# Five small moves in a two-layer encoder trunk: a put-off GpSimd product, one more row transposition before a stage border, weight splits kept to odd steps for longer, and two changes of order

## The chip, the cores and the metric

The kernel runs on one core of a Trainium2 chip. The metric is the device time of one execution in microseconds (us). Shown are three runs of the kernel before (median 1502.16 us) and one profiled execution of it. The engines are named as in the profile: PE (matrix multiplications and transpositions), PEld (its weight loads), DVE (vector), ACT (scalar, activations), POOL (GpSimd) and SP (which here only starts transfers).

## The reference, cut to what matters

The trunk has two layers over 1024 tokens of width 1024, all in fp32. Layer 0 uses neighbourhood attention (mixer A), layer 1 grouped-query attention (mixer B); both have 16 query heads of width 64.

```python
# one layer
h    = rms_norm(x, g)
proj = h @ w_in                       # q, k, v and a gate of the branch's width
o    = mixer(q, k, v)                 # A: window of 8 x 16 keys plus a bias; B: 4 kv heads, rotary, all 1024 keys
x    = x + (o * silu(gate)) @ w_out
x    = x + sigmoid(rms_norm(x) @ w_gate) * (p[i] @ w_ple)
# after both layers
out  = rms_norm(x, g_final)
```

The product of `o` and the gate is where the first edit sits. The attention output is scaled by 1 / (row sums), and by the gate, and is then the left operand of the output projection.

## The kernel before, in words

**Products.** Each fp32 operand is split into a high half and a low half, and a product is three matmuls (high by high, high by low, low by high), recorded under line L322. A split takes an ACT copy (the high half) and a DVE subtraction (the low half). Weight blocks of 128 x 1024 are staged by SP into `wstage`, split by ACT at L231 and DVE at L236, and queued in an object `WQ`. Rows of activations are turned by four PE transpositions into one PSUM bank `t` (L504), which ACT copies to `HTh` (L505) and DVE subtracts to `HTl` (L506). `to_ht(pool, tile, rows, halves)` does this for one tile of 128 tokens, once per half of the row.

**Stages.** Mixer A runs from about 65 to 515 us, its dense stage (the output projection by seven half-size products after Strassen, then the gated embedding) to about 694, mixer B to about 1319 and the second dense stage to the end.

**Order of work.** The order on each engine is the order in which the program is written. Attention items are woven with projections ("dense" items). `post.add(n, f)` puts off `f` by `n` pulses, and one pulse passes per woven item; `post.tick()` counts. `later` does the same per attention step.

**The end of a head pair (edit 1).** `head_end` collects a pair of heads in `Y` (128 x 512), once for each half `hf` of the queries. Row sums are inverted, sent through memory and spread by SP (`rD`, `rb`). Then `fin` multiplies on GpSimd twice: `Y` by the gate `G` (L611) and `Y` by `rb` (L612). Eleven pulses later `split` makes the high half on ACT (L608) and the low half on DVE (L609), and two transfers store them; for `pair < 4` and `hf == 1`, `Y` is stored as it is after 13 pulses. In mixer A the same GpSimd queue holds, once per step of eight, L831 for `PTh` and for `PTl` (the products that mask the outer columns of the turned probabilities), for which PE's product `o<-PTh,V` and `o<-PTl,V` waits; also L773 (the bias of the next head) and the transfers of L680 that add weight blocks for the Strassen sums. For the last pair, `fin_last` does the products on DVE, and `hi` and `lo` write directly into `HTh` (L589) and `HTl` (L592); for `hf == 0` they are put off by 3 and 5 pulses (edit 2).

**Steps of mixer B (edit 3).** 128 steps `n`. A step does scores `s`, their minimum (DVE L1311), the exponential (ACT L1317), eight transpositions (L1329), whose banks ACT (L1331) and DVE (L1332) split; every even step does two steps' product with `V` (L322, `o<-PTh,V` and `o<-PTl,V`, eight matmuls each). `WQ.gate` is false in even steps up to step 111, so that no weight split is made there; from step 112 it is open. Late in mixer B, at L654, ACT evacuates the products `d` of the embedding projection.

**The dense stage (edit 4).** `strassen_out` holds a table `plan` that gives, for each tile product, the additions (`s12`, `s3`: two or four DVE instructions at L1487 to L1495), copies (`sh`, L1505; `sl`, L1509) and weight splits (`wh`, L1457; `wl`, L1461) made after it.

**The border to mixer B (edit 5).** The dense stage keeps a list `pend` of row halves still to be turned. What is left at its end is handed to mixer B, which turns one of them after every second of its first projection items, into its own pool `psT`. That pool takes over the PSUM banks of the dense stage's pool `ps_t`, so that its first transpositions wait for the DVE instruction that last read such a bank. The items there are `k` and `v` products of 24 matmuls each into `s` (L322), evacuated by ACT (L1249, L1255).

Of the kernel before, what the change touches and what calls it, by code (L numbers as in the profile page):

```python
# [16 lines left out]
ALU = mybir.AluOpType  # L17
# [31 lines left out]
QO = (4, 6)  # L49
AGE, LAG = 3, 3  # L50
YS = (11, 11)
YLOAD_A, YLOAD_B = 0, 118
OPEN3 = 5
ULOAD = 5
# [107 lines left out]
def trunk(ctx, tc, x, wts, rpb, gains, hgains, mask, sides, rope, gain0, out):  # L162
    nc = tc.nc
    sync, act, dve, pool, pe = nc.sync, nc.scalar, nc.vector, nc.gpsimd, nc.tensor
# [97 lines left out]
    WQ = Weights()  # L262
# [56 lines left out]
    post = Later()  # L319
# [195 lines left out]
    def head_end(sb, h, hf, rs, Ops, ylive, layer, gg, talloc):  # L515
        pair = h // 2
        b = (h % 2) * 64
        if h % 2 == 0:
            Y = sb.tile([128, 512], F32, name="Y", bufs=3 if layer == 0 else 2)
            rb = sb.tile([128, 512], F32, name="rb", bufs=2)  # L520
            r8 = sb.tile([128, 8], F32, name="r8", bufs=4)
            ylive[pair, hf] = (Y, rb, r8, {})
        Y, rb, r8, tail = ylive[pair, hf]
        yh = Y[b:b + 64]

        def join():
            dve.scalar_tensor_tensor(yh, Ops[0:64], 0.5, yh, op0=ALU.mult, op1=ALU.add)

        def rows():
            r8T = sb.tile([128, 32], F32, name="r8T", bufs=2)  # L530
            dve.transpose(r8T.rearrange("p (a c) -> p a c", a=4), r8[:, None].to_broadcast([128, 4, 8]))
            rD = dram.tile([8, 128], F32, name="rD", bufs=4)
            for b in range(4):
                post.add(DD[layer][1], lambda b=b: sync.dma_start(rD[:, 32 * b:32 * b + 32], r8T[32 * b:32 * b + 8]))
            for i in range(2):
                post.add(DD[layer][1], lambda i=i: sync.dma_start(
                    rb[64 * i:64 * i + 64], bass.AP(tensor=rD.tensor, offset=rD.offset + 512 * i, ap=[[0, 64], [1, 512]])))

        def spread():
            dve.tensor_copy(rb.rearrange("p (t j c) -> p t j c", t=4, j=2),  # L540
                            r8.rearrange("p (j t) -> p t j", j=2)[:, :, :, None].to_broadcast([128, 4, 2, 64]))

        def across():
            ps = talloc()
            for t in range(4):
                pe.transpose(ps[:, t], rb[:, t * 128:(t + 1) * 128], ident)
            ps = ps.rearrange("p t c -> p (t c)")
            if hf == 0:
                act.activation(rb, ps, AF.Copy)
            tail["rb"] = rb if hf == 0 else ps  # L550

        def norm():
            if "sums" in tail and h % 2:
                post.add(DT[hf], across)
                return
            dve.reciprocal(r8[:, 4 * (h % 2):4 * (h % 2) + 4], rs)
            if h % 2 == 0:
                return
            if pair < 7 or layer == 1 and hf == 0:
                post.add(DD[layer][0], rows)  # L560
                tail["rb"] = rb
            else:
                spread()
                post.add(DT[hf], across)

        def evac():
            act.activation(yh, Ops[64:128], AF.Copy, scale=0.5)
            post.add(DY, join)
            norm()
        if h == NH - 1 and hf == 1:  # L570
            evac()
        else:
            post.add(DO[layer], evac)
        if h % 2 == 0:
            return None
        G = gg.pop((pair, hf))
        del ylive[pair, hf]

        def fin_last():
            dve.tensor_tensor(Y, Y, G, ALU.mult)  # L580
            if "rb" not in tail:
                post.l = [e for e in post.l if e[1] is not across]
                across()
            dve.tensor_tensor(Y, Y, tail["rb"], ALU.mult)
            y3 = Y.rearrange("p (t c) -> p t c", t=4)
            ts = slice(4 * hf, 4 * hf + 4)

            def hi():
                act.activation(HTh[:, ts, 7, :], y3, AF.Copy)  # L589

            def lo():
                dve.tensor_tensor(HTl[:, ts, 7, :], y3, HTh[:, ts, 7, :], ALU.subtract)  # L592
            if hf == 0:
                post.add(3, hi)
                post.add(5, lo)
            else:
                hi()
                lo()

        def fin():  # L600
            yhi, ylo = rb.bitcast(F32R), Y.bitcast(F32R)

            def store(c, src):
                sync.dma_start(yD[layer][c][4 * hf:4 * hf + 4, :, pair, :].rearrange("t p c -> p t c"),
                               src.rearrange("p (t c) -> p t c", t=4))

            def split():
                act.activation(yhi, Y, AF.Copy)  # L608
                dve.tensor_tensor(ylo, Y, yhi, ALU.subtract)  # L609
                post.add(2, lambda: (store(0, rb), store(1, Y)))  # L610
            pool.tensor_tensor(Y, Y, G, ALU.mult)  # L611
            pool.tensor_tensor(Y, Y, rb, ALU.mult)  # L612
            if pair < 4 and hf == 1:
                post.add(YS[layer] + 2, lambda: store(0, Y))
            else:
                post.add(YS[layer], split)
        return fin_last if pair == 7 else fin
# [477 lines left out]
    def mixer_b(pend):  # L1095
        with ExitStack() as es:
# [283 lines left out]
            for g in range(4):  # L1380
                att = []
                for n in range(32 * g, 32 * g + 32):
                    h, hf, t = steps[n]
                    av = n >= 2 and n % 2 == 0
                    w = CB if av else CN
                    def turn():
                        if WQ.gate:
                            WQ.gate = False
                        later.tick()
                    att.append((turn, w[0]))  # L1390
                    if av:
                        att.append((lambda n=n: f_AV(*steps[n - 1]), w[1]))
                    te = [(blocks(n), w[2])]
                    if n + 1 < len(steps):
                        te.append((exps(n + 1), w[3]))
                    if n % 2 == 0 and n > 0:
                        te.reverse()
                    att += te
                    if n + 2 < len(steps):
                        def scores(n=n):  # L1400
                            f_S(*steps[n + 2])
                            WQ.gate = n % 2 == 1 if n < 112 else None
                        att.append((scores, w[4]))
                    m = n + QS_AT
                    if m % 8 == 0 and m < len(steps):
                        hn, fn, _ = steps[m]
                        att.append((lambda hn=hn, fn=fn: turned.append(lambda: q_stack(hn // 2, fn)), 0.0))
                    if YLOAD_B <= n < YLOAD_B + NT:
                        att.append((lambda t=n - YLOAD_B: load_y(1, t), 0.0))
                if g == 3:  # L1410
                    def last():
                        end[0] = 1
                        f_AV(*steps[-1])
                    att.append((last, CB[1]))
                def gates(p):
                    return [i for hf in range(2) for i in gate_items("bg", p, hf, dalloc, sb, gg)]
                dense = []
                if g > 0:
                    dense += left
                if g < 3:  # L1420
                    qi = q_items(g + 1, pool)
                    kv = kv_items(1, pool) if g == 1 else [None, None]
                    dense += kv[:-2] + qi[:KS] + [k for k in kv[-2:-1] if k] + qi[KS:8] + [k for k in kv[-1:] if k] + gates(2 * g + 1) + qi[8:]
                    left = gates(2 * g + 2)
                else:
                    WQ.cap[3] = 2
                    dense += gates(2 * g + 1) + pp_items(1, dalloc, sb, TAGS_B)
                mix(att, dense, hold=HOLD + 1 if g == 3 else 0)
# [6 lines left out]
    def strassen_out(l, X, ps_d, ps_t, early):  # L1435
# [87 lines left out]
        for t in range(4):  # L1523
# [3 lines left out]
            1: [(sh, "s2", 0), (s12, 1), (s3, 1)],  # L1527
            2: [(sl, "s2", 0), (sh, "s2", 1)],
            3: [(sl, "s2", 1), (s12, 2)],
            4: [(wh, "t2", 0), (wh, "t2", 1), (s3, 2)],  # L1530
            5: [(wl, "t2", 0), (wl, "t2", 1), (sh, "s2", 2), (fetch_raw, "t4", 0), (fetch_raw, "t4", 1)],
            6: [(sl, "s2", 2), (s12, 3)],
            7: [(s3, 3), (sh, "s2", 3), (wh, "t3", 0)],
            8: [(sl, "s2", 3), (wl, "t3", 0), (wh, "t3", 1), (sh, "s3", 0)],
# [79 lines left out]
    def dense_phase(l):  # L1614
        with ExitStack() as es:
# [9 lines left out]
            pend = []  # L1625
# [93 lines left out]
            for kind in ("ple",):  # L1719
# [3 lines left out]
                for hf in range(2):  # L1723
# [77 lines left out]
                    for t, i in order:  # L1801
# [39 lines left out]
                        for i, (u, xn) in enumerate(grp):  # L1841
# [3 lines left out]
                            else:  # L1845
                                pend += [(clock[0] + 3, u, xn, (c,)) for c in range(2)]
            WQ.cap[2] = WQ.cap[4] = 0
            return [p[1:] for p in pend]

    def rope_tables(sb):  # L1850
# [46 lines left out]
```

## Time and profile before

| | |
|---|---|
| three runs | 1500.39, 1502.16, 1502.37 us |
| profiled execution | 1500.79 us, of which the span is 1499.0 us |
| granted TensorE clock, mean | 0.998 |
| PE, DVE, ACT, POOL busy | 1478.6, 1069.6, 916.3, 445.2 us |
| mixer A (65 to 515 us): PE busy | 448.2 of 450 us |
| dense stage of layer 0 (515 to 694): PE busy | 177.7 of 179 us |
| mixer B (694 to 1319): PE busy | 619.2 of 625 us |
| dense stage of layer 1 (1319 to the end): PE busy | 172.4 of 180 us |

A row of a timeline gives the start, the duration, the engine, the line and operation with output <- inputs, how many instructions the row stands for, and in brackets how long the engine stood idle just before and what ended it. Busy PE time is modelled: a matmul of 512 columns has a duration of 0.39 us in the rows while the next one starts 0.23 us later. So where PE waits, the distance between two starts tells more than the idle figure.

### The profile page before, as it was taken

The page shows a single profiled execution, that of the slowest core. Times are in us where ns is not written, and L with a number is a line of the kernel's source. Part 1 is how long each engine was busy: PE and PEld are TensorE (multiplying, and loading weights), DVE is VectorE, ACT ScalarE, POOL GpSimd, SP SyncE. Part 2 cuts the span into 40 slices and gives each one's busy share as a digit, 9 for nine tenths or more (in the row PEclk, how much of TensorE's full clock was granted, in tenths as well). Part 3 has the DMA queues.
Part 4 walks back from the last instruction along what each step waited for, and adds up shares of the span by engine and source line. Part 5 has one row for each costly group of instructions (what it writes and reads, how often), then busy time and mean ns, then how long its engine had stood idle before and what let it go on. Part 6 is the DMA issues. An engine that isn't in the chain of part 4 may idle for free.

```text
span 1499.0 us, 24720 instructions
## 1 busy us (share of the span) xinstructions
PE 1478.6 (99%) x8881; PEld 1302.8 (87%) x8881; DVE 1069.6 (71%) x2027; ACT 916.3 (61%) x1860; POOL 445.2 (30%) x637
## 2 busy tenths in 40 slices
PE   8999999999999999999999999999999999999997
PEld 8888988988988888888988999989999988888886
DVE  6666476477477598756887786777877787789845
ACT  6676476477477535433567776666767777745432
POOL 3355475387265200020322122443130300000000
PEclk9999999999999999999999999999999999999999
DMA  8424374283132862262210111111111122763223
GB/s 263 140 93 127 81 167 138 64 171 97 36 89 85 328 247 99 92 207 80 77 50 22 33 48 42 47 33 43 59 28 48 38 78 64 246 234 108 79 98 128
DMA packets 91466, 157.70 MB, mean 105 GB/s; under 512 B 18256, under 2 KB 54352, under 8 KB 90832
## 3 DMA queue, kind: packets, MB, share of 16 engines
q1 hardware_dynamic: 87344, 143.80, 28.9%
q0 software_dynamic: 2560, 8.39, 3.7%
q10 hardware_dynamic: 1440, 3.94, 0.8%
q8 instruction: 71, 1.16, 0.3%
q14 instruction: 51, 0.42, 0.1%
HBM read 125.56 MB, written 50.83 MB: 118 GB/s over the span
## 4 chain that ended last, share of the span: by engine, by line
PE 86%; DVE 6%; DMA 3%; ACT 2%; issue 1%; POOL 1%; SPq 1%; DVEq 0%; POOLq 0%; ACTq 0%
PE d L322 53%; PE s L322 11%; PE o L322 11%; PE t L1329 7%; PE t L821 2%; PE t L504 2%; DMA HTl<-yD0l 1%; DMA X<-in_x 1%; DVE wl L236 1%; PE t L322 1%; DVE PTl L1332 1%; DVE mn L1311 0%; PE t L1281 0%; DMA ppD<-G 0%; DVE xn L1674 0%
## 5 line engine op out<-in xcount | busy, mean ns | idle before, releaser
L322 PE MATMUL d<-wh,HTh 128*128 128x256 f32 (+1 forms) x1000 | 330.7, 335 | 0.3 <-ACT G L654 0.2
L322 PE MATMUL d<-wh,HTl 128*128 128x256 f32 (+1 forms) x1000 | 326.8, 331 | 0.5 <-DVE HTl L506 0.5
L322 PE MATMUL d<-wl,HTh 128*128 128x256 f32 (+1 forms) x1000 | 325.9, 330 | 0.6 <-DVE wl L1461 0.6
L1332 DVE TENSOR_TENSOR PTl<-t,PTh 128x512 fp32r<-128x512 f32 x256 | 164.6, 685 | 104.5 <-ACT PTh L1331 104.2
L322 PEld LDWEIGHTS d<-wl,HTh 128*128 128x128 f32 x1000 | 187.6, 189 | 20.2 <-DVE wl L1461 1.0
L322 PEld LDWEIGHTS d<-wh,HTh 128*128 128x128 f32 x1000 | 187.4, 189 | 19.9 <-ACT G L654 0.5
L322 PE MATMUL d<-HTh,wh 128*128 128x512 f32 x504 | 204.6, 406 | 0.0
L322 PEld LDWEIGHTS d<-wh,HTl 128*128 128x128 f32 x1000 | 187.5, 189 | 19.1 <-DVE HTl L506 0.9
L322 PE MATMUL d<-HTh,wl 128*128 128x512 f32 x504 | 198.1, 393 | 0.0
L322 PE MATMUL d<-HTl,wh 128*128 128x512 f32 x504 | 197.3, 392 | 0.0
L1317 ACT ACTIVATE P<-s,mn 128x1024 f32<-128x1024 f32 x128 | 142.9, 1117 | 47.9 <-DVE mn L1311 46.9
L1331 ACT ACTIVATE PTh<-t 128x512 fp32r<-128x512 f32 x256 | 139.4, 594 | 45.7 <-PE t L1329 45.2
L1311 DVE TENSOR_REDUCE mn<-s 128x1 f32<-128x1024 f32 x128 | 155.0, 1211 | 9.7 <-PE s L322 9.2
L831 POOL TENSOR_TENSOR PTh<-PTh,SIDE 128x256 fp32r<-128x256 f32 x96 | 81.4, 848 | 194.2 <-ACT PTh L826 194.1
L1329 PE MATMUL t<-ident,P 128*128 128x128 f32 x1024 | 134.9, 273 | 2.6 <-DVE PTl L1332 2.0
L322 PE MATMUL s<-KA,QS 128*128 128x512 f32 (+2 forms) x384 | 134.0, 403 | 0.0
L1329 PEld LDWEIGHTS t<-ident,P 128*128 128x128 f32 x1024 | 115.3, 140 | 12.9 <-DVE PTl L1332 7.1
L322 PE MATMUL s<-KB,QS 128*128 128x512 f32 (+2 forms) x384 | 121.5, 370 | 0.0
L322 PE MATMUL o<-PTl,V 128*128 128x256 f32 (+2 forms) x672 | 120.2, 290 | 1.1 <-DVE PTl L1332 0.6
L322 PE MATMUL o<-PTh,V 128*128 128x256 f32 (+2 forms) x672 | 118.3, 287 | 2.6 <-POOL PTh L831 1.3
L236 DVE TENSOR_TENSOR wl<-wstage,wh 128x1024 fp32r<-128x1024 f32 x79 | 98.1, 1243 | 29.3 <-ACT wh L231 29.0
L322 PEld LDWEIGHTS d<-HTh,wl 128*128 128x128 f32 x504 | 94.6, 188 | 21.6
(272 smaller groups left out, 2860.9 us busy)
## 6 DMA issues: line engine op xcount, KB each, us to landing
wstage<-in_wts SPq DMA_DIRECT2D x88, 512.0 KB
pp<-ppD SPq DMA_DIRECT2D x32, 256.0 KB
X<-in_x SPq DMA_DIRECT2D x15, 512.0 KB
rb<-rD SPq DMA_DIRECT2D x58, 128.0 KB
ppD<-th SPq DMA_DIRECT2D x20, 256.0 KB
tD0t<-in_wts SPq DMA_DIRECT2D x16, 256.0 KB
tD1t<-in_wts SPq DMA_DIRECT2D x16, 256.0 KB
xD<-X SPq DMA_DIRECT2D x8, 512.0 KB
```

The source lines that it names most:

```text
L236: eng.tensor_tensor(lo[:, c:c + n], s[:, c:c + n], hi[:, c:c + n], ALU.subtract)
L322: pe.matmul(ps, a, b, start=first, stop=last, skip_group_check=True)
L504: pe.transpose(ps[:, k], xn[:, (4 * c + k) * 128:(4 * c + k + 1) * 128], ident)
L821: pe.transpose(ps[:, i], sp[:, c * 128:(c + 1) * 128], ident)
L831: pool.tensor_tensor(pt[:, 3 * j - 1:3 * j + 4:4], pt[:, f1:f1 + 1].to_broadcast([128, 2, 128]), SIDE[:, :2], ALU.mult)
L1311: dve.tensor_reduce(mn, ps, axis=AX.X, op=ALU.min)
L1317: act.activation(p, ps, AF.Exp, bias=mn, scale=-1.0, accum_out=RS[h, hf][:, t:t + 1])
L1329: pe.transpose(ps[:, i], p[:, k * 128:(k + 1) * 128], ident)
L1331: act.activation(PTh[:, ks, c], ps, AF.Copy)
L1332: dve.tensor_tensor(PTl[:, ks, c], ps, PTh[:, ks, c], ALU.subtract)
```

## The change

1. `fin` no longer does the second GpSimd product at once: it is put off by `YD = 6` pulses. Everything else of `fin` keeps its pulses.
2. In `fin_last`, for `hf == 0`, the low half is put off by 8 pulses and not 5.
3. Weight splits stay out of even steps of mixer B up to step 121, not 111.
4. In the table `plan`, `s3` of tile 2 moves from entry 4 to entry 5, behind the two low halves of the weight block `t2`.
5. At the end of the dense stage, one more element of `pend` is turned there, into a bank of `ps_t`. Layer 1's dense stage ends with `pend` empty.

```diff
+YD = 6
@@ fin_last
             if hf == 0:
                 post.add(3, hi)
-                post.add(5, lo)
+                post.add(8, lo)
@@ fin
             pool.tensor_tensor(Y, Y, G, ALU.mult)
-            pool.tensor_tensor(Y, Y, rb, ALU.mult)
+            post.add(YD, lambda: pool.tensor_tensor(Y, Y, rb, ALU.mult))
             if pair < 4 and hf == 1:
                 post.add(YS[layer] + 2, lambda: store(0, Y))
@@ mixer_b
-                            WQ.gate = n % 2 == 1 if n < 112 else None
+                            WQ.gate = n % 2 == 1 if n < 122 else None
@@ strassen_out, plan
-            4: [(wh, "t2", 0), (wh, "t2", 1), (s3, 2)],
-            5: [(wl, "t2", 0), (wl, "t2", 1), (sh, "s2", 2), (fetch_raw, "t4", 0), (fetch_raw, "t4", 1)],
+            4: [(wh, "t2", 0), (wh, "t2", 1)],
+            5: [(wl, "t2", 0), (wl, "t2", 1), (s3, 2), (sh, "s2", 2), (fetch_raw, "t4", 0), (fetch_raw, "t4", 1)],
@@ dense_phase
             WQ.cap[2] = WQ.cap[4] = 0
+            if pend:
+                to_ht(ps_t, *pend.pop(0)[1:])
             return [p[1:] for p in pend]
```

One line is added near the top of the file, so the changed kernel's lines are one higher from there on (three higher at its end): L612 becomes L613, L831 becomes L832, L506 becomes L507.

On GpSimd in mixer A, this stood at the end of a pair's second half (Y by the gate at L611, Y by the sums at L612, transfers of L680, the masked probabilities at L831, the next bias at L773), before:

```order
L831 TENSOR_TENSOR PTl<-PTl,SIDE 128x2x128
L611 TENSOR_TENSOR Y<-Y,G 128x512
L612 TENSOR_TENSOR Y<-Y,rb 128x512
L680 DMA tD0t_83<-tD0t_82 64x1024
L831 TENSOR_TENSOR PTh<-PTh,SIDE 128x2x128
L831 TENSOR_TENSOR PTl<-PTl,SIDE 128x2x128
L680 DMA tD0t_83<-tD0t_82 64x1024
```

and this stands there now:

```order
L832 TENSOR_TENSOR PTl<-PTl,SIDE 128x2x128
L612 TENSOR_TENSOR Y<-Y,G 128x512
L681 DMA tD0t_83<-tD0t_82 64x1024
L832 TENSOR_TENSOR PTh<-PTh,SIDE 128x2x128
L832 TENSOR_TENSOR PTl<-PTl,SIDE 128x2x128
L681 DMA tD0t_83<-tD0t_82 64x1024
L613 TENSOR_TENSOR Y<-Y,rb 128x512
L681 DMA tD0t_85<-tD0t_83 64x1024
```

The pair of L831 now passes the second product, and with it the wait for `rb`. All 14 such places of mixer A move in this way; at the end of a pair's first half the product then stands right ahead of the following pair of L831.

On DVE at the border from the dense stage to mixer B (L1842 writes the last two normalised rows, L506 the low half of a transposition, L1158 belongs to mixer B's first k product), before:

```order
L357 SCALAR_TENSOR_TENSOR stn<-wkn 128x2
L1842 SCALAR_TENSOR_TENSOR wstage<-X_6047,stn,gain 128x1024
L1842 SCALAR_TENSOR_TENSOR wstage<-X_6048,stn,gain 128x1024
L506 TENSOR_TENSOR HTl<-t,HTh 128x512
L1158 TENSOR_REDUCE ss<-t_7559 128x2
```

and now:

```order
L358 SCALAR_TENSOR_TENSOR stn<-wkn 128x2
L1843 SCALAR_TENSOR_TENSOR wstage<-X_6047,stn,gain 128x1024
L1843 SCALAR_TENSOR_TENSOR wstage<-X_6048,stn,gain 128x1024
L507 TENSOR_TENSOR HTl<-t,HTh 128x512 x2
L1159 TENSOR_REDUCE ss<-t_7566 128x2
```

The low half of the added transposition is the first of the two L507: it stands behind both long L1843, although its transposition is made on PE before mixer B's first product.

On DVE at a weight split late in mixer B (L527 joins a head's output, L236 is the low half of the weights, L531 turns the sums), before:

```order
L527 SCALAR_TENSOR_TENSOR Y<-o,Y 64x512
L236 TENSOR_TENSOR wl_14334<-wstage,wh_14333 128x1024
L1332 TENSOR_TENSOR PTl<-t,PTh 128x4x128 x2
L531 STREAM_TRANSPOSE r8T<-r_14140 128x32
L1311 TENSOR_REDUCE mn<-s 128x1
```

and now:

```order
L528 SCALAR_TENSOR_TENSOR Y<-o,Y 64x512
L1333 TENSOR_TENSOR PTl<-t,PTh 128x4x128 x2
L532 STREAM_TRANSPOSE r8T<-r_14139 128x32
L1312 TENSOR_REDUCE mn<-s 128x1
L237 TENSOR_TENSOR wl_14371<-wstage,wh_14370 128x1024
```

The weight split goes behind the step's own two splits and its minimum. Two splits move in this way (at 1256 and 1289.7 us of the profile before); all others stay.

## The prediction

> **What bounds the kernel now.** I read the engine shares first, then what PE waited for, then single stretches.
>
> ```profile
> PE 1478.6 (99%) x8881; PEld 1302.8 (87%) x8881; DVE 1069.6 (71%) x2027; ACT 916.3 (61%) x1860; POOL 445.2 (30%) x637
> ```
>
> PE works nearly all the time, and no edit takes a matmul away. So a gain can only come out of PE's waits, and the list of these says how little there is: longest first, each row with the sum in us, the count, and the longest.
>
> ```profile
> PE o L322 <- POOL PTh L831: 1.3, 2, 1.0
> PE s L322 <- ACT th L1249: 0.9, 1, 0.9
> PE o L322 <- DVE Y L527: 0.8, 2, 0.5
> PE t L504 <- DVE HTl L506: 0.7, 3, 0.3
> ...
> PE o L322 <- DVE PTl L1332: 0.6, 1, 0.6
> PE d L322 <- DVE wl L1461: 0.6, 1, 0.6
> ```
>
> Each edit aims at one of these rows: the first at L831, the second at L527, the third at L1332, the fourth at L1461, the fifth at L1249. I take them one by one; a price is the distance between two PE starts beyond the usual one.
>
> **Edit 1, the put-off GpSimd product.** GpSimd around a pair's second half in mixer A, then PE there:
>
> ```profile
> 191.59 1.78 POOL L611 TENSOR_TENSOR Y<-Y,G 128x512 f32<-128x512 f32 x1
> 194.30 1.30 POOL L612 TENSOR_TENSOR Y<-Y,rb 128x512 f32<-128x512 f32 x1 [0.93 <-DMA rb<-rD]
> 195.54 0.78 POOL L680 DMA_DIRECT2D tD0t<-tD0t  x1
> 196.09 0.98 POOL L831 TENSOR_TENSOR PTh<-PTh,SIDE 128x256 fp32r<-128x256 f32 x1
> 196.78 0.97 POOL L831 TENSOR_TENSOR PTl<-PTl,SIDE 128x256 fp32r<-128x256 f32 x1
> ```
>
> ```profile
> 196.39 0.40 PE L322 MATMUL d<-HTh,wl 128*128 128x512 f32 x1
> 197.12 0.45 PE L322 MATMUL o<-PTh,V 128*128 128x384 f32 x1 [0.34 <-POOL PTh L831]
> ```
>
> ```profile
> 315.32 0.40 PE L322 MATMUL d<-HTh,wl 128*128 128x512 f32 x1
> 316.73 0.44 PE L322 MATMUL o<-PTh,V 128*128 128x384 f32 x1 [1.01 <-POOL PTh L831]
> ```
>
> GpSimd waited 0.93 us for `rb`, multiplied, and only then masked the probabilities. PE's next matmul came 0.73 us after the last instead of 0.23 (0.50 lost), and at the second place 1.41 instead of 0.23 (1.18 lost). At both, the low half's matmul behind it loses as much again as the second mask takes longer, about 0.5, and the transposition behind that 0.1. The sum is 0.5 + 0.5 + 0.1 + 1.2 + 0.5 + 0.1 = 2.9 us; the idle column alone, which counts modelled ends, would give some 1.8. Without the product and its wait the pair starts 1.30 + 0.93 us earlier, near 193.9, and ends at about 195.4, while PE asks for it at 196.62. So all of it goes: **-2.9**, with 1.2 us to spare. The product itself then runs behind the pair, about 195.9 to 197.2, where `rb` has landed, and is read by the split only some five pulses on; the bias L773, at 198.5 before, is not later. Only the transfer that stores `Y` unsplit is up to 1.8 us later, and that is read in the dense stage, a hundred us away. In mixer B the product changes places with other work at three places, where no PE row waits for GpSimd's products.
>
> A two-input DVE instruction slows down where it meets such a product: L628 took 1.65 us at 314.09 and takes 0.69 alone (the median of its 32).
>
> ```profile
> 314.09 1.65 DVE L628 SCALAR_TENSOR_TENSOR G<-th,G 128x512 f32<-128x512 f32 x1 [0.81 <-ACT th L624]
> ```
>
> The Trainium skill (SBUF — State Buffer, Who interferes with whom) says that a DVE instruction with two SBUF inputs and a GpSimd one that reads SBUF exclude each other for a whole instruction, which the 1.65 agrees with. By that rule a moved product blocks another DVE instruction in its new place, by up to its own 1.3 us and not by the 0.96 of this row, and the sum would be the same as long as PE does not wait for that one. PE's list for mixer A has 0.2 us behind DVE in all, so I charge nothing.
>
> **Edit 3, the weight split out of an even step.**
>
> ```profile
> 1255.29 0.69 DVE L527 SCALAR_TENSOR_TENSOR Y<-o,Y 64x512 f32<-64x512 f32 x1
> 1256.00 1.23 DVE L236 TENSOR_TENSOR wl<-wstage,wh 128x1024 fp32r<-128x1024 f32 x1
> 1257.15 1.28 DVE L1332 TENSOR_TENSOR PTl<-t,PTh 128x512 fp32r<-128x512 f32 x2
> ```
>
> ```profile
> 1256.12 1.18 PE L322 MATMUL o<-PTh,V 128*128 128x256 f32 x8 [0.31 <-DVE Y L527]
> 1257.88 1.33 PE L322 MATMUL o<-PTl,V 128*128 128x256 f32 x8 [0.58 <-DVE PTl L1332]
> ```
>
> PE's second eight start 1.76 us after the first, where eight take 0.96 (0.119 each, by the 24 that take 2.88 below), and run 0.2 longer while the second L1332 ends: 0.94 lost to L236, which stood ahead of them on DVE and now stands behind. The wait for L527 ahead of it stays. The second moved split costs less: its L1332 run to 1292.26 beside eight matmuls that take 1.34 and not 1.11, so 0.2.
>
> ```profile
> 1290.64 1.11 PE L322 MATMUL o<-PTh,V 128*128 128x256 f32 x8
> 1291.72 1.34 PE L322 MATMUL o<-PTl,V 128*128 128x256 f32 x8
> ```
>
> Both splits now stand ahead of the next odd step's L1332, for which DVE was idle 1.8 us in the second case. **-1.1** together; bounds 0 (they hold up the next step as much) and -1.2.
>
> **Edit 2, the last head's low half.** It stood ahead of L527, and PE's `o` waited for that (0.5 of the row of 0.8 in the list).
>
> ```profile
> 1305.53 0.68 DVE L592 TENSOR_TENSOR HTl<-Y,HTh 128x512 fp32r<-128x512 f32 x1
> 1306.13 0.68 DVE L527 SCALAR_TENSOR_TENSOR Y<-o,Y 64x512 f32<-64x512 f32 x1
> ```
>
> Now L527 and both L1332 come first, and `o` starts 0.6 earlier. But DVE works without a gap from 1304.4 to 1309.1, and the minimum at the end of that run releases the exponential and, behind it on ACT, the evacuation that PE's `d` at 1311.22 waits for:
>
> ```profile
> 1310.57 0.60 ACT L654 ACTIVATE th<-d 128x512 f32<-128x512 f32 x1
> ```
>
> ```profile
> 1311.22 0.50 PE L322 MATMUL d<-wh,KA 128*128 128x512 f32 x1
> ```
>
> The same instructions stand ahead of that minimum as before, so it comes no earlier and PE waits there instead: **-0.1**, between 0 and -0.6.
>
> **Edit 4, the order in the dense stage.** PE waited for the low weights at 538.57 (0.8 by starts), behind the two `s3` additions of 0.7 us each.
>
> ```profile
> 535.00:549.20 14.20, 13.64 (x61) 10.93 (x60) 13.99 (x20) 6.16 (x10) 0.00 (x0) 1.00 0.73 276
> ```
>
> In that window the DVE column (the third) is busy 13.99 of 14.20 us, and it goes on so until about 580. What is put behind the weights delays what follows by as much, and PE needs `HTl` of `s3` at 549.0, when it was just ready. The wait moves there: **-0.1**, between +0.1 and -0.8. In layer 1 the same rows show no such wait.
>
> **Edit 5, the added transposition.** The chain of waits over the border (start, us, what):
>
> ```profile
> 694.60 3.14 PE s L322 x24
> 697.73 0.44 PE t L504 x4
> 698.17 2.88 PE s L322 x24
> ...
> 701.92 0.39 ACT th L1249
> 702.32 0.04 issue
> 702.36 3.14 PE s L322 x24
> ```
>
> It fills the 0.41 us before 694.60, in which PE waited for ACT (four transpositions take 0.44). But it takes a bank of the dense stage, which mixer B's next transposition, the one at 697.73, has to write. That one waits for the last reader of the bank. Before, this was an L506 done at 696.6. Now it is the added L506, which on DVE stands behind both L1842:
>
> ```profile
> 698.47 2.48 DVE L1842 SCALAR_TENSOR_TENSOR wstage<-X,stn,gain 128x1024 f32<-128x1024 f32 x2
> ```
>
> So it ends near 698.47 + 2.48 + 0.65 = 701.6. PE stands from 697.6 to 701.6, then does four transpositions (0.44), 24 matmuls (2.88), four more transpositions (0.44), and begins the third product at 705.4 and not 702.36: 3.0 later, with one transposition more behind it (0.44). Net **+2.6**. The wait for L1249 vanishes in it, since ACT now evacuates during the 24 matmuls. Bounds: +3.1 if the saved transposition is lost again, and -1.4 if nothing held it: then the gap of 0.41 and the wait of 1.0 before 702.36 would both be used.
>
> **Sum.** -2.9 - 1.1 - 0.1 - 0.1 + 2.6 = **-1.6 us**. The sum is made against the profiled execution's own 1500.79, which gives 1499.2. Its time lies 1.4 below the median of the three runs, within which the executions scatter by 2; from the median it gives 1500.6, from the mean of all four executions (1501.4) 1499.8. I say **1500.2**.
>
> **The rivals.**
>
> *Nothing holds the transposition* (another bank is free, or its low half is earlier). For it: PE shows no wait at 697.7 today. Against it: the added L506 is written behind the L1842 pair. It would give -2.9 - 1.1 - 0.2 - 1.4 = -5.6, hence 1496.5. Chance 0.12.
>
> *The dense and the last-head orders keep their gains*, 0.8 and 0.6, since DVE catches up before the next need. Against it: the full DVE windows. -1.6 - 1.2 = -2.8, hence 1499.3 from the median. Chance 0.13.
>
> *The masks stay late*, because they wait for something other than the product, or edit 3 gives back its gain in the next step. For it: only two of 14 places showed a wait, so the timing there is close. Sum +1.3 without edit 1; 1503.4. Chance 0.11.
>
> *Slower: the put-off product blocks the next mask pair.* At a first half it now stands right ahead of the pair, seven times in mixer A, each with 1.3 us of GpSimd.
>
> ```profile
> 186.53 0.99 POOL L831 TENSOR_TENSOR PTl<-PTl,SIDE 128x256 fp32r<-128x256 f32 x1
> ```
>
> ```profile
> 190.42 0.28 PE L322 MATMUL o<-PTh,V 128*128 128x256 f32 x1
> ```
>
> This pair ended at 187.5 and was needed at 190.42; behind a product it ends at 188.8, with 1.6 to spare. Where the distance is under 1.3, PE waits; it decides if the seven places lose 0.7 us each on the mean, 4.9 in all, which would give +3.3 and 1505.5. Against it are the 1.6 us. Chance 0.08.
>
> **How the numbers follow.** The forecast as summed has the remaining 0.56. A measurement of this kernel can tell about 0.2%, 3.0 us, from no change. Faster by more means under 1499.2: all of the first rival, half of the second, and about a tenth of the forecast's 0.56, together 0.25. Slower by more is the last rival, 0.08. The rest, 0.67, cannot be told from no change. The range runs from the first rival's 1496.5 to the third's 1503.4, which leaves out the slower one and the edges. The forecast's own range is 1499 to 1502.
>
> **What would show it.** Edit 1: no PE row behind L831 near 197 and 316, and the product between the mask pair and the bias. Edit 3: `o<-PTl` 0.96 after `o<-PTh` near 1258. Edit 5: a row of PE's waits of about 4 us, transposition behind L506, near 701; if that row is missing, the first rival holds. Edits 2 and 4: new waits near 1311 and 549 of the size of those gone. What would make the forecast wrong above all is the size of edit 5, since it takes back most of what the others give.

## The result, and the profile after

The changed kernel is slower: 1504.31 us median (1503.11 to 1506.43, 21 runs) against 1501.81 us, a ratio of 1.0015 with a 95% interval of 1.0009 to 1.0021, or +2.3 us (+1.4 to +3.2). That is below the 0.2% that was set as the bound of what can be told, but clear of zero, and outside the predicted range. The profiled execution has a span of 1501.8 us against 1499.0. All ratios compare fast runs alone; one execution of one experiment (the low half ahead of the norm), of 6584.22 us, is left out as slow.

What PE waited for in the changed kernel, longest first (us in total, times, longest):

```profile
PE t L505 <- DVE HTl L507: 4.6, 4, 3.9
PE t L1330 <- DVE PTl L1333: 2.7, 4, 1.0
PE t L822 <- DVE PTl L828: 1.4, 2, 0.7
```

The row of 1.3 us behind the masks (L831) is gone, and so are those behind L1332 (for `o`), L1461 and L1249; of the 0.8 us behind L527, 0.3 are left. In their place stand 3.9 us behind the low half of a transposition, 0.7 more than before at L1330, and 1.4 us at L822, which the kernel before did not have. The row of L1330 was the longest before, and the list in the prediction leaves it out:

```profile
PE t L1329 <- DVE PTl L1332: 2.0, 3, 0.9
```

To see where the time went, the same PE matmul is looked up in both traces, and the difference of its two starts is followed through the program. It moves at these places:

| place (us, before) | edit | step of the difference, us | predicted |
|---|---|---|---|
| 197, 316: masks at the second halves | 1 | -0.5 -0.5 -0.1 and -1.2 -0.5 -0.1 | -2.9 |
| 191, 310: transposition L821 at the first halves | 1 | +0.84 and +0.85 | 0 |
| 321: scores behind them | 1 | +0.4 | 0 |
| 538: low weights, given back until 588 | 4 | -0.8, then +0.5 | -0.1 |
| 697 to 716: border to mixer B | 5 | -1.1 before it, +3.0 after it: +4.1 | +2.6 |
| 1258 and 1292: the moved splits | 3 | -0.9 and -0.3 | -0.9, -0.2 |
| 1296: transposition L1329 | 3 | +0.9 | 0 |
| 1307 and 1311: last head's low half | 2 | -0.6, +0.3 | -0.1 |

These make +2.4; a step of -0.3 at 489 us, which edit 1 alone shows too, and +0.6 in small steps between 740 and 1002 us make up most of the rest of the +2.8 by which the two spans differ. Three losses were not in the prediction: the border costs 1.5 us more, the first halves lose 1.7 us, and one step after the second moved split loses 0.9.

**The border.** DVE, then PE, in the changed kernel; the last two rows are windows (us, then busy time of PE, PEld, DVE, ACT and POOL, then the granted clock, DMA share and GB/s):

```profile
697.35 2.48 DVE L1843 SCALAR_TENSOR_TENSOR wstage<-X,stn,gain 128x1024 f32<-128x1024 f32 x2
699.74 0.68 DVE L507 TENSOR_TENSOR HTl<-t,HTh 128x512 fp32r<-128x512 f32 x1
```

```profile
700.49 1.04 PE L505 MATMUL t<-ident,xn 128*128 128x128 f32 x4 [3.88 <-DVE HTl L507]
```

```profile
701.00:704.10 3.10, 3.10 (x17) 3.10 (x16) 0.89 (x3) 1.47 (x5) 0.00 (x0) 0.51 0.13 36
704.10:707.00 2.90, 2.90 (x26) 2.90 (x26) 1.09 (x6) 1.39 (x5) 0.00 (x0) 1.00 0.14 40
```

The order is as predicted: the low half stands behind both L1843, and PE waits 3.9 us for it (4.0 was forecast). But the work behind the wait runs at a granted clock of 0.51 until 704: 17 matmuls in 3.1 us, where the next 2.9 us hold 26.

**The first halves.** The DVE copy L779 (L780 after) in head 4, before and after:

```profile
186.10 1.59 DVE L779 COPY_PREDICATED tb<-SIDE,tb 128x128 f32<-128x128 int32 x1
```

```profile
186.35 2.83 DVE L780 COPY_PREDICATED tb<-SIDE,tb 128x128 f32<-128x128 int32 x1
```

and GpSimd there in the changed kernel, and what PE then waits for:

```profile
186.06 1.56 POOL L613 TENSOR_TENSOR Y<-Y,rb 128x512 f32<-128x512 f32 x1
187.33 0.99 POOL L832 TENSOR_TENSOR PTh<-PTh,SIDE 128x256 fp32r<-128x256 f32 x1
188.02 0.98 POOL L832 TENSOR_TENSOR PTl<-PTl,SIDE 128x256 fp32r<-128x256 f32 x1
```

```profile
191.93 0.41 PE L822 MATMUL t<-ident,sp 128*128 128x128 f32 x2 [0.68 <-DVE PTl L828]
```

The copy ends at 189.18, just after the third GpSimd instruction (189.00). Before, only the two masks ran beside it, and it ended at 187.69. Everything behind it on DVE is later, a weight split of 1.2 us, L609 and then the low half L827, whose bank PE needs.

### The profile page after: what moved, and what is told of

Read it like the earlier page. It is cut to its first block, busy times and chain, and to the rows that moved or that the text cites. A ratio compares the mean times of both kernels' runs of the same rounds, so it can differ in the third digit from the quotient of the medians.

```text
span 1501.8 us, 24698 instructions
## 1 busy us (share of the span) xinstructions
PE 1479.8 (99%) x8881; PEld 1305.2 (87%) x8881; DVE 1077.4 (72%) x2027; ACT 916.1 (61%) x1860; POOL 443.7 (30%) x637
## 4 chain that ended last, share of the span: by engine, by line
PE 47%; DVE 3%; ACT 2%; issue 1%; POOL 0%; DMA 0%; DVEq 0%; POOLq 0%; ACTq 0%
PE d L323 22%; PE s L323 9%; PE o L323 8%; PE t L1330 7%; PE t L323 1%; DVE PTl L1333 1%; PE t L505 1%; DVE mn L1312 1%; PE t L1282 0%; ACT P L1318 0%; ACT PTh L1332 0%; DVE wl L237 0%; DVE QS L1292 0%; ACT wh L232 0%; POOL qt L1180 0%
## 5 line engine op out<-in xcount | busy, mean ns | idle before, releaser
L1332 ACT ACTIVATE PTh<-t 128x512 fp32r<-128x512 f32 x256 | 139.4, 594 | 46.7 <-PE t L1330 46.2
L832 POOL TENSOR_TENSOR PTh<-PTh,SIDE 128x256 fp32r<-128x256 f32 x96 | 82.3, 857 | 196.3 <-ACT PTh L827 196.3
L1330 PE MATMUL t<-ident,P 128*128 128x128 f32 x1024 | 135.0, 273 | 3.3 <-DVE PTl L1333 2.7
L1330 PEld LDWEIGHTS t<-ident,P 128*128 128x128 f32 x1024 | 115.2, 140 | 14.0 <-DVE PTl L1333 8.2
```

The costliest lines, as they stand in the source:

```text
L832: pool.tensor_tensor(pt[:, 3 * j - 1:3 * j + 4:4], pt[:, f1:f1 + 1].to_broadcast([128, 2, 128]), SIDE[:, :2], ALU.mult)
L1330: pe.transpose(ps[:, i], p[:, k * 128:(k + 1) * 128], ident)
L1332: act.activation(PTh[:, ks, c], ps, AF.Copy)
```

## The experiments

Each kernel below is the kernel before with the edit shown, unless it says otherwise; each was timed in five rounds against the kernel before on the same chip, whose median there was 1501.6 or 1501.7 us. A trace shows one execution, and not always a usual one: those of the kernel without edit 5 and of the two with added GpSimd work took 2.1 to 4.5 us more than the median of their kernel. So places are compared there, not whole spans.

### Edit 5: the added transposition

**Edit 5 alone**

```diff
             WQ.cap[2] = WQ.cap[4] = 0
+            if pend:
+                to_ht(ps_t, *pend.pop(0)[1:])
```

> Edit 5 alone, on the kernel before. Theory A, from the changed kernel's trace: PE waits about 3.9 us for the added low half, and the 15 or so matmuls after the wait come 0.21 us apart instead of 0.12 (the granted clock there was 0.51), so the edit costs about 4.1 us by itself: +4.1 against before. The prediction's own sum, without the clock, said +2.6. The rival that nothing holds the transposition says -1.4.

Measured: ratio 1.0025 (1.0015 to 1.0035), +3.8 us; in the trace the border costs +4.1. It is the whole loss and more. The chain of waits over the border and the window behind it:

```profile
700.97 0.61 DVE HTl L506
701.58 0.05 issue
701.63 0.66 PE t L504 x4
702.28 4.37 PE s L322 x24
```

```profile
702.00:705.20 3.20, 3.20 (x20) 3.20 (x19) 0.94 (x4) 1.47 (x5) 0.00 (x0) 0.59 0.17 49
```

The 24 matmuls of the second product take 4.37 us, against 2.88 before.

**Edit 5 with PE kept busy through the wait**

```diff
+                        if i == 0 and t == 0:
+                            for _ in range(34):
+                                mm(pro_s[-1][:, 512:768], HTh[:, 0, 0, :], WQ.get(("bkv", 0, 0))[0][:, :256], True, True)
                         act.activation(kv, ps, AF.Copy)
```

(`pro_s` keeps the tile of the first product.)

> Edit 5 alone, and 34 extra matmuls of 256 columns written behind mixer B's first k product, into a part of its bank that nobody reads; they fill about 4 us of PE's wait and change nothing else. Theory A (the matmuls behind the wait are slow because PE stood still and the clock was halved): the 24 matmuls of the second product take 2.9 us and not 4.0, and the kernel is at about +2.6 against before although PE does more work. Rival (they are slow for another reason, such as the transfers or the rows that they read): they stay at 0.21 us each, and the time stays at +4.1 or rises.

Measured: 1.0019 (1.0010 to 1.0027), +2.9 us. In its chain the 24 matmuls behind the 58 (24 and the 34 added) take the usual time, and the granted clock of the window is 1.00:

```profile
698.10 7.03 PE s L322 x58
705.12 0.46 PE t L504 x4
705.58 2.88 PE s L322 x24
```

```profile
705.00:709.00 4.00, 4.00 (x37) 4.00 (x36) 1.41 (x6) 1.94 (x7) 0.00 (x0) 1.00 0.12 35
```

So the slow stretch was the clock after PE had stood still, and not the rows or transfers. At the border this kernel loses 2.6 us in its trace, the prediction's own figure, against 4.1 with edit 5 alone, with 34 matmuls more. By the two ratios it gains 0.9 on edit 5 alone, which their intervals do not separate; the two traces, of one execution each, do.

**Edit 5 with the low half ahead of the norm**

```diff
+                        if l == 0 and t == NT - 1 and pend:
+                            to_ht(ps_t, *pend.pop(0)[1:])
                         r = norm_r(sb, sq, grp[0][0], len(grp))
```

> Edit 5 with the added transposition written ahead of the last norm, so that its low half stands on DVE ahead of the two long L1842 rows and not behind them; on PE it stands where edit 5 puts it. Theory A (the wait is for that one low half, late only by its place on DVE): no wait before mixer B's second transposition, granted clock 1.0, and -0.4 to -1.4 us against before. Rival (the bank hand-over itself holds PE, whichever place the low half has): +4.1, as edit 5.

Measured: 0.9997 (0.9988 to 1.0006), -0.5 us, not to be told from no change nor from -1.4; in its trace the border is at +0.3. The wait for the low half is 0.4 us and not 3.9, so the hand-over as such costs little, and it was the place on DVE. In the trace the hoped-for gain does not come: the wait for L1249 is back (0.9 us). The chain from there:

```profile
702.96 0.45 PE t L504 x4
703.41 0.06 issue
703.47 0.04 ACTq L1249
...
703.91 0.39 ACT th L1249
704.30 0.04 issue
704.35 1.69 PE s L322 x12
```

The added low half stands ahead of the norm, the L1842 pair (L1844 there) starts at 700.91, 2.7 us after the sum of squares of its norm where it was 1.7, and L1249 starts only when the L1842 pair is done (at 703.39). What is won on PE is lost there: at neither of the two places tried has edit 5 anything to give at this border, as long as L1249 waits for that pair.

**The change without edit 5**

> The change without edit 5. Theory A: the other four edits together are worth -1.4 us (the changed kernel's trace is 1.1 us ahead just before the border; after it they gain 1.0 and lose 0.7 again): -1.4 against before. The prediction's sum for the same four says -4.2.

Measured: 0.9981 (0.9972 to 0.9990), -2.9 us (-4.2 to -1.5). The two expectations, -1.4 and -4.2, lie at the two ends of the interval, which does not decide between them. Against the full change (+2.3) edit 5 makes a difference of 5.1 between the ratios, against 3.8 alone. Its trace shows the steps of the table, with 1.6 (0.5 and 1.1) and not 0.4 at 321.

### Edit 1: the put-off product

**Edit 1 alone**

> Edit 1 alone. Theory B, from the changed kernel's trace: the two old waits for the masks go (-2.7), but in the first half of heads 4 and 8 the put-off product meets the DVE copy L779, which then takes 2.8 us and not 1.6; DVE's rows behind it slip, and PE waits twice 0.85 us for the low half L827 (+1.7), with 0.4 more in the step behind: -0.6 against before. The prediction said -2.9; its slower rival (the next mask pair is blocked) would show PE's waits behind L831 and not behind L827.

Measured: 0.9987 (0.9978 to 0.9996), -2.0 us (-3.3 to -0.6). The interval reaches from the prediction's -2.9 to the -0.6 expected here, so the time alone does not decide. In its trace +0.87 and +0.86 come at 191 and 310, and -1.1 and -1.8 at 197 and 316, which is what was expected. The 0.4 at 321 does not come here, and it was 1.6 in the kernel without edit 5; what sets it is not shown.

**One more GpSimd product at the first halves, nothing moved**

```diff
             pool.tensor_tensor(Y, Y, rb, ALU.mult)
+            if hf == 0 and layer == 0:
+                scr = sb.tile([128, 512], F32, name="scr", bufs=1)
+                post.add(6, lambda: pool.tensor_tensor(scr, Y, rb, ALU.mult))
```

> The kernel before with both products at once, and in mixer A, at the first halves, one more GpSimd product (Y by rb, 128 x 512) 6 pulses later into a tile that nobody reads: GpSimd reads SBUF at the moment at which edit 1 does. Theory B (a GpSimd instruction that reads SBUF shuts out the DVE copy): L779 at heads 4 and 8 goes from 1.59 to about 2.8 us, PE waits twice 0.85 us, +1.7 to +2 us. Rival (the masks come late because GpSimd's queue is longer): the waits are behind L831.

Measured: 1.0011 (1.0000 to 1.0022), +1.7 us, just at the edge of what can be told from no change. In the trace +0.86 comes at 191 and again at 310. The copy takes as long as with edit 1, and the two waits for L827 (here L830) are in the list of mixer A, with the sum of 1.4 that the full change has:

```profile
186.84 2.85 DVE L782 COPY_PREDICATED tb<-SIDE,tb 128x128 f32<-128x128 int32 x1
```

```profile
PE o L322 <- POOL PTh L834: 3.6, 2, 2.5
PE t L824 <- DVE PTl L830: 1.4, 2, 0.7
```

The first row, 3.6 us, is the old wait for the masks at the second halves, 1.3 before, which edit 1 would remove. That it is longer here need not be this kernel's doing: the wait differs between executions (last section). So the trace shows the price of the longer copy, 2 x 0.86, and the time by itself does not.

**Memsets in the place of that product**

```diff
-                post.add(6, lambda: pool.tensor_tensor(scr, Y, rb, ALU.mult))
+                post.add(6, lambda: (pool.memset(scr, 0.0), pool.memset(scr, 0.0)))
```

> As the run with the extra product, but the extra GpSimd work is two memsets of a 128 x 512 tile, which write and read nothing. Theory B in the form of the Trainium skill's page (SBUF - State Buffer, Who interferes with whom: the contention is with GpSimd instructions that read): L779 stays at 1.6 us, the two PE waits do not come, +0. Rival (any GpSimd work in that place delays DVE or the masks): L779 grows by the length of the memsets, and the waits come, +1 to +2.

Measured: 1.0023 (1.0013 to 1.0033), +3.5 us, against an expectation of 0. On the copy the expectation holds, and by more than was said: GpSimd is just as busy there (1.37 us, no inputs), and the copy takes 0.30, its shortest.

```profile
186.44 1.37 POOL L615 MEMSET scr<- 128x512 f32 x2
187.78 0.75 POOL L834 TENSOR_TENSOR PTh<-PTh,SIDE 128x256 fp32r<-128x256 f32 x1
```

```profile
186.73 0.30 DVE L782 COPY_PREDICATED tb<-SIDE,tb 128x128 f32<-128x128 int32 x1
...
191.11 3.06 DVE L747 SCALAR_TENSOR_TENSOR QS<-th,QS 64x512 fp32r<-64x512 f32 x1
```

```profile
PE s L322 <- DVE mn L806: 2.8, 2, 1.4
PE o L322 <- POOL PTh L834: 2.4, 2, 1.7
```

But the masks and all that follows on GpSimd stand later, and now meet another DVE instruction with SBUF inputs, L744 (here L747): it takes 3.06 us, 0.80 before, beside the next masks and L611, and PE waits twice for what is behind it. So the wait for L827 did not come, as the theory said, and two others did, which it had not looked for. It is not shown that work on GpSimd in that place could be free; it is shown that work that reads nothing does not lengthen the copy beside it.

**Edit 1 at the second halves only**

```diff
-            pool.tensor_tensor(Y, Y, rb, ALU.mult)
+            if hf:
+                post.add(YD, lambda: pool.tensor_tensor(Y, Y, rb, ALU.mult))
+            else:
+                pool.tensor_tensor(Y, Y, rb, ALU.mult)
```

> Edit 1 for the second halves only; at the first halves the product stays at once. Theory B: the waits at 197 and 316 us go, those at 191 and 310 do not come: -2.3 to -2.7 us. Rival (the loss of edit 1 comes from the second halves, or the gain from the first): between -0.6 and +1.

Measured: 0.9977 (0.9968 to 0.9986), -3.5 us (-4.8 to -2.1); in its trace the difference to the kernel before goes by -2.9 at 197 and 316, and nothing comes at 191 and 310. What is left of PE's waits in mixer A is one row:

```profile
PE d L323 <- ACT G L658: 0.2, 1, 0.2
```

### Edits 2, 3 and 4

**Edit 3 alone**

> Edit 3 alone. Theory C, from the changed kernel's trace: the first moved split gains 0.75 us; the second gains 0.1 but shifts the turn of the transfers' completion signals, so that the last load of HTl on ACT's queue waits for a transfer that started 2.9 us later, ACT stands behind it, and PE waits 0.6 for a split in the next step (+0.8): -0.1 against before in all. The prediction said -1.1.

Measured: 1.0001 (0.9992 to 1.0010), no change. In its trace -0.9 at 1258, +0.3 at 1268, -0.3 at 1292 and +0.8 at 1296. ACT behind the second moved split, where the queue's own row is the start of a load of `HTl`:

```profile
1290.38 1.07 ACT L231 ACTIVATE wh<-wstage 128x1024 fp32r<-128x1024 f32 x1
1292.66 0.33 ACTq L286 DMA_DIRECT2D HTl<-yD1l  x1
1293.11 0.60 ACT L654 ACTIVATE th<-d 128x512 f32<-128x512 f32 x1 [1.66 <-PE t L1329]
```

ACT is done at 1291.45, and stands until it may issue the load at 1292.66. In the full change the same load is issued at 1295.61, and the transfer that it waits for, the `HTl` load of 1290.67, had landed at 1295.59. In the kernel before, it waits for another one, which started at 1287.75 and landed at 1291.58, and is issued at 1291.60, when ACT has only just finished. In the semaphore records of the traces the load waits for signal 107 in the kernel before and for signal 110 in the other two. The reading that fits is that each transfer takes one of a few completion signals in turn and waits for the last one that used it, so that with one transfer moved this load's turn falls on a later one; the order of the turns was not traced any further. The row's releaser (`PE t`) is a guess of the profile: PE had nothing to do with it.

**Edit 3 up to step 116: only the first split moves**

```diff
-                            WQ.gate = n % 2 == 1 if n < 112 else None
+                            WQ.gate = n % 2 == 1 if n < 116 else None
```

> Edit 3 with the bound at step 116 and not 122: only the first of the two splits moves. Theory C: -0.75 us, and no wait of ACT for the HTl load near 1295. Rival (the loss near 1299 comes from the first moved split): it stays, and the sum is near 0.

Measured: 0.9995 (0.9986 to 1.0004), -0.8 us by the ratio, which five rounds do not tell from none; its trace has the -0.9 at 1258 (and +0.2 at 1268) and not the +0.8, and ACT issues the load where it ends its own work, as before.

```profile
1291.94 0.21 ACT L1317 ACTIVATION_READ_ACCUMULATOR P<-s,mn 128x1 f32 x1
1291.98 0.33 ACTq L286 DMA_DIRECT2D HTl<-yD1l  x1
1292.43 0.60 ACT L654 ACTIVATE th<-d 128x512 f32<-128x512 f32 x1 [0.28 <-ACT P L1317]
```

**Edits 2 and 4 alone**

> Edits 2 and 4 alone. From the changed kernel's trace: edit 4 takes 0.8 us off the wait for the low weights and gives back 0.3 in the next 50 us, edit 2 takes 0.6 and gives back 0.35: -0.7 in all. The prediction said -0.2 (all given back); the rival that both gains are kept says -1.4.

Measured: 1.0000 (0.9991 to 1.0009). In its trace edit 4 has -0.8 at 538 and then +0.8 in three steps at 550, 577 and 588, and edit 2 -0.60 and then +0.35: given back whole and by more than half, as the prediction had it. The time fits that (0.0, with -1.4 at the very edge of the interval), but does not tell -0.2 from -0.7.

### The parts that gain, together

Edit 1 at the second halves, edit 3 up to step 116, edits 2 and 4, and no edit 5:

> Edit 1 at the second halves only, edit 3 to step 116, edits 2 and 4 as they are, no edit 5. If the parts add: -2.7 - 0.75 - 0.7 = -4.1 us against before, about 1497.6. If the parts get in each other's way (a wait that moves on): no better than edit 1 at the second halves alone, -2.7 to -3.4.

Measured: 1496.72 us median (1496.31 to 1497.69, 6 runs), ratio 0.9968 (0.9956 to 0.9979), -4.8 us (-6.6 to -3.2). It is faster than the kernel before, and by the two ratios than the changed one. The interval holds the expected -4.1 and, at its edge, the -3.4 of parts that get in each other's way. The span of its profiled execution is 1494.5, 4.5 below that of before, by the steps already seen: -2.9 (edit 1), -0.9 (edit 3), -0.3 (edit 2), -0.4 between 538 and 588, and some tenths between them. The -0.4 need not be edit 4's: edit 1 alone, and edit 1 at the second halves only, have -0.4 at 538 too.

## Why the prediction was wrong

The forecast was -1.6 us and the change costs +2.3. The four parts measured alone (+3.8, -2.0, +0.2, 0.0) add to +2.0, so within their intervals nothing shows that they act on each other, and the error can be read edit by edit.

**Edit 5, the mis-sized term.** The mechanism was right: the bank hand-over, the place of the low half behind both L1842, the wait of 4.0 (3.9 measured). The step "then does four transpositions (0.44), 24 matmuls (2.88)" failed: it took the rates of a PE at full clock for one that had just stood still for 4 us. At the granted 0.51 they took 1.0 and 4.0 us in the changed kernel. The term is +4.1 and not +2.6, above the upper bound of +3.1 that was stated, and the experiment that kept PE busy took this part away (+2.6). The longest waits between the matmuls of the trace of before were about 1 us once the stages ran, so the price behind one of 4 us was not there to read. But that the clock falls when PE stands could be read there: PE's last matmul starts at 1491.11, and the end of the span has

```profile
1493.90:1499.00 5.10, 0.00 (x0) 0.00 (x0) 1.08 (x3) 0.72 (x1) 0.00 (x0) 0.50 0.27 103
```

with a granted clock of 0.50. The bound should have allowed for it. The rival that nothing holds the transposition fell.

**Edit 1, the sentence "so I charge nothing".** The gain at the second halves was -2.9, as summed. The loss of +1.7 at the first halves was missed. The prediction had the mechanism in its hands, with L628 at 1.65 us beside a product and the rule of the Trainium skill (SBUF — State Buffer, Who interferes with whom) that the two engines exclude each other, and dismissed it because PE's list for mixer A showed only 0.2 us behind DVE. That list says what DVE is late for now, not how much slack it has: behind the copy of 186.10 stood, before, 2.3 us of DVE work with one gap of 0.34, and the low half L827 was done at 190.18, 0.65 before PE needed it at 190.83. That makes 1.0 us of cover. In its new place the product lengthens the copy by 1.24 and, since the masks behind it move too, L609 from 0.68 to 1.23: 1.8 in all, and 0.8 is what PE waited. The cover could have been read from the rows of before, had it been looked up which DVE instruction the product would meet; the 1.24 and the slower L609 in part only. The runs agree with the rule on what it says of reading (2.85 us beside a product, 0.30 beside memsets). They do not agree with one whole instruction as the bound of the loss, as the prediction took it: the copy did not get in between three GpSimd instructions in a row.

The slower rival named the right place, the first halves, and the wrong victim: the masks end at 189.0, near the 188.8 worked out, and PE asks for them at 190.7 with time to spare. DVE was the victim, at two of the seven places.

**Edit 3, a queue that was not followed.** -0.9 at the first split was right. The second split gains 0.3 and loses 0.9 in the next step, behind an ACT-queue load that now waits for another, later transfer. With that edit 3 makes about -0.4 in the changed kernel's trace and not -1.1, and alone +0.2 (-1.2 to +1.5) by the time: not to be told from either of the stated bounds, 0 and -1.2. The reason given for 0 was another one. The order of the queues was compared for the moved split and not for the waits of later transfers.

**Edits 2 and 4** were right in kind. Edit 2's 0.6 comes back by half at 1311, as named (-0.3 net against -0.1, within its bounds). Edit 4's 0.8 comes back whole when the two are alone, though only by a third at the place named (550); in the full change 0.5 comes back, at 577 and 588, and the 0.35 that stay are there with edit 1 alone too.

Of the rivals, none was it: the change came out slower by edit 5's clock and edit 1's DVE copy together, each of them 1.5 to 1.7 us. One half of the third rival came true beside them, that edit 3 gives back its gain in the next step, by a mechanism that the prediction did not have.

## What to carry to other kernels

When an instruction of GpSimd is moved, list what DVE does in the new place, and count the DVE work without a gap from there to the next thing that PE needs: that, and not the list of PE's waits, is the cover. A wait of PE of some microseconds can cost more than its length; either keep it short or fill it. An instruction that a hand-over of memory waits for should be written ahead of long work on its engine, since the wait is on the place in the queue and not on the data; but look at what the long work then holds up, as L1249 here.

## What the runs showed of the hardware that was not expected

**The half clock follows waits of two to four microseconds, but not each of them.** After the 3.9 us of the border the granted clock was 0.50 for 3.4 us (700.6 to 704.0). In the run with the extra product PE stood 2.5 us for the masks in head 8 (2.9 from start to start), and then:

```profile
321.49 0.69 PE L322 MATMUL o<-PTh,V 128*128 128x384 f32 x1 [2.51 <-POOL PTh L834]
```

```profile
321.40:325.00 3.60, 3.51 (x9) 2.67 (x10) 0.42 (x1) 0.87 (x3) 3.60 (x10) 0.50 0.88 128
```

while a start-to-start distance of 2.4 us at the same place (2.0 idle), in the run with the early low half, left the clock at 1.00 in the window behind it:

```profile
318.10:321.50 3.40, 3.12 (x15) 2.60 (x16) 0.68 (x2) 0.88 (x3) 3.40 (x8) 1.00 1.13 196
```

A shorter one, 2.3 us (1.9 idle), in the run with PE kept busy, did halve it:

```profile
318.44 0.44 PE L322 MATMUL o<-PTh,V 128*128 128x384 f32 x1 [1.88 <-POOL PTh L831]
```

```profile
320.16:323.57 3.41, 3.41 (x11) 2.94 (x10) 1.15 (x4) 0.60 (x3) 3.41 (x9) 0.50 0.93 136
```

So the length of a wait does not decide alone. In the clock records of these traces the clock changes only at whole steps of 3.413 us: from the first record of full clock to the first fall behind a wait it is 692.91 us (203 steps) in the changed kernel, 310.61 (91) with PE kept busy, and 314.03 (92) with the extra product and with the memsets. Counted within one such step, PE was idle 3.3, 1.7, 1.9 and 1.7 us where the clock fell at the step's end; with the early low half the 2.0 us lie across two steps, 1.5 and 0.5, and it did not fall. That fits all of them, but no run was made to test it, and it does not say why the slow stretch lasted two steps with the extra product and one elsewhere.

The Trainium skill (TensorE: Matmul & The Clock Gate, What's actually happening) has the clock halved after an idle window of about 3.4 us and full again after a busy one, by a window that runs freely. The steps agree with that, and so does the length of the slow stretch at the border; waits of 1.9 and 2.5 us that halve it are shorter than the stated window.

**A DVE instruction can be shut out by a row of GpSimd instructions.** L779 took 0.30 us beside memsets, 1.59 beside two masks and 2.83 beside a product and two masks, in the last two cases ending shortly after the last of them.

**The wait for the masks at the second halves is not one size.** In kernels that leave edit 1 out, PE's distance at 316 was 1.4 us in the profiled execution of before, 2.3 and 2.4 in those of two of edit 5's kernels, since GpSimd waited 1.6, 2.5 and 2.6 us for `rb` ahead of the product. Part of the scatter of the kernel before may sit there, in the wait and in the half clock behind it: in the comparison with edit 1 at the second halves its 31 runs lie 6.2 us apart (1500.76 to 1506.93), the 11 with that edit 2.4 (1497.40 to 1499.78). In the three comparisons 10 of its 89 runs had a mean granted clock of 0.997 or less, and these took 1502.66 us or more, where the median of the others was 1501.5; of the 39 runs of the four kernels that move the product at the second halves and leave edit 5 out, none was under 0.998. That could also be why edit 1 at the second halves gains 3.5 by the time and 2.9 in the trace. That this is the cause was not tried.
